# A two-layer hybrid trunk on one core: another order of the seven products, a longer estimate for accumulating loads, six output tiles by token halves, and an interleaved MLP norm

## The chip, the core and the metric

The kernel runs on one core of a Trainium2 chip. Its time is the device time of one execution in microseconds (us). Before the change, three runs took 2100.82 to 2105.32 us, median 2102.74 us.

## What is computed

The reference is one inference step of a two-layer trunk with 128 context tokens and 512 latent tokens, 640 in all, of width 1024. The part that matters here is the end of a layer: the output projection with its gated residual, the second RMSNorm with a modulation, and a squared-ReLU MLP of width 4096.

```python
def _block(x, cond, lp, lam, lam_scale, ctx):
    mod = (jax.nn.silu(cond) @ lp["w_ada"] + lp["b_ada"])[:, None, :]
    sh1, sc1, g1, sh2, sc2, g2 = jnp.split(mod, N_MOD, axis=-1)
    h = _rms_norm(x, lp["norm1_g"]) * (1 + sc1) + sh1
    m, new_kv = _mixer(h, lp, lam, lam_scale, ctx)
    x = x + g1 * m
    h = _rms_norm(x, lp["norm2_g"]) * (1 + sc2) + sh2
    f = jnp.square(jax.nn.relu(h @ lp["w_mlp1"])) @ lp["w_mlp2"]
    return x + g2 * f, new_kv
```

`_mixer` (four token mixers and their gated merge) ends in `merged @ lp["w_out"]`, and its work is not touched. Context and latent tokens have different conditioning vectors, so the modulation differs between tokens 0 to 127 and the rest.

## The kernel before

**Layout and arithmetic.** Activations are feature-major: 128 features in the partitions, 640 tokens along the free dimension, cut into two token halves of 320 (`HALVES`). Each fp32 operand is held as a rounded high part and a low part, and each product of two operands is three matmuls: high by high, low weight by high, high weight by low (`mm3`). So each weight tile of 128x1024 needs a cast on ScalarE (`whi`) and a subtraction on VectorE (`wlo`) before use, and each activation likewise (`hh` and `hl`, `p5h` and `p5l`, and so on).

**Stream of weights (`Stream`, `W`).** Weights are added in the order of use. Row 0 goes through four slots of high and low parts (`NSLOT`), row 1 through two half slots, row 2 has a buffer of its own, given with `own` (line 279). The raw data come through a ring of four raw slots; a slot is reloaded when its weights were split. `load` (240) issues a plain load on SyncE's queue and, for `more`, an accumulating load on GpSimd's queue that adds a second block of weights to the first.

**Seven products.** Three of four MLP-1 and MLP-2 steps per layer (`q` 0 to 2), and the fourth MLP-1 step, are 2x2 block products done with seven multiplications instead of eight (`square_chunks`, 540, and `block`, 2027). A product has four output tiles of 320 tokens, 48 matmuls. p1, p6, p7 and p4 add up in PSUM banks 0 to 3; p2, p5 and p3 in banks 4 to 7. p2 starts the second group, p5 starts it anew, and p3 adds to it. After each product `results` (2049) reads a group: p1, p5 and p6 are copied by ScalarE (`ev`), p2, p3 and p7 are added to such a copy by VectorE (`fq`, or `ev` in MLP-2 and the last MLP-1), p4 is read directly. The order is `ORDER` (538): p1, p2, p5, p6, p3, p7, p4. The weights of p5, p6 and p3 are sums that follow from each other: they stay in two buffers (`chain`), and each is made from the one before by one accumulating load, which is issued when the earlier one was split. p7's weights come through the raw ring, a plain load and an accumulating one.

The operands are made by `sums` (1917) from four quarters of the input, in the order p5, p6, p3, p7, p4, each waiting for units in `room` (1897). In MLP-1 the operands are used for all four `q`; those of p7 and p4 are spilled to DRAM (`put_away`, 1952) and reloaded on SyncE's queue for `q` 1 to 3 (`load_again`, 1956), called by `before` (2223) at the start of p6 (for p7) and of p3 (for p4).

**Order of work.** The order of instructions on each engine is fixed at build time by a planner that runs along with the code. `Clocks.put` (95) keeps an estimated time for each engine and buffer. A DMA is estimated by

```python
            end = max(self.t[eng], start + 1100.0) + cost(n)
        ...
        seen = end + (900.0 if eng == "dma" else self.LAG)
```

with a cost of bytes / 360 in ns. `pump` (329) puts the next weight cast in ScalarE's queue when its source is estimated to be there, and the subtraction in VectorE's. Generators in eight `lanes` hold the other work; `tick` (614), called after every two contraction steps of matmuls, steps those that are due, lower lanes first. Engines run their queues in order. `until` forces pending work when TensorE's next product has no operand.

**Units.** SBUF buffers are 30 units of 128x1280 words (`NUNIT`); a unit asked for when none is free forces pending work.

**End of a layer's first half.** The output projection has eight output tiles. `units_of` (1862) does tiles 0 to 3, each with both token halves; `tail` (828) does tiles 4 to 7 for the first half and then for the second. After each tile `x_update` adds it to the residual on VectorE and `sq_add` adds its square, ScalarE then VectorE. After each half `tail` starts `mlp_norm(part)` (1969), the first in lane 2, the second in lane 3: sums over features by TensorE (`ones`), a reciprocal square root on VectorE, a broadcast by TensorE (`ident`), a copy to `rb`, then for each of eight feature tiles a multiply on VectorE (`ht`, split at token 128 in the first half) and an activation with the shift as bias on ScalarE (`hq`); in the first half, after each pair, a cast `hh` and a subtraction `hl`, which are the operands of p1 and p2. The sums for p5 need the second half.

The trace puts every operation on one line (131), that of the wrapper, so groups are told apart by tile names.

## Time and profile before

| | |
|---|---|
| three runs | 2100.82, 2102.74, 2105.32 us |
| profiled execution | 2096.17 us |
| its span, first to last instruction | 2094.4 us |
| mean granted TensorE clock | 0.988 |
| busy: PE, DVE, ACT, POOL | 2017.3, 1325.9, 1002.9, 212.7 us |
| output projection and MLP of layer 0 | about 552 to 1030 us of the span |
| the same of layer 1 | about 1577 to 2094 us |
| HBM read | 277.92 MB |

PE is TensorE's matmuls, PEld its weight loads, DVE VectorE, ACT ScalarE, POOL GpSimd, SPq SyncE's queue. In a table of stretches each engine has its busy time and, in brackets, its number of instructions; PEclk is the granted clock. A row of waits has the total, the number of waits and the longest. A timeline row has start, duration, the instruction, and in square brackets the idle time before it and what ended it. A row of a group has the busy time, the mean ns of one, and the idle time before.

### The profile page before, as it was taken

Reading aid. Unit: us, or ns where it says so; the run is one execution under the profiler, and the core shown is the slowest. Engines: PE = TensorE matmul, PEld = TensorE weight load, DVE = VectorE, ACT = ScalarE, POOL = GpSimd, SP = SyncE. Lnnn points to the kernel's source line nnn. Section 1 sums busy time; section 2 is a strip of 40 time slices with the busy share of each in tenths; the row PEclk is TensorE's granted clock in tenths of the full one; section 3 lists DMA queues with packets and bytes.
Section 4 is the critical chain, followed back from the end, with each engine's and each line's share of the span. In section 5 each row is a group of like instructions: output and inputs, shape, how many; then the busy total and the mean of one; then the engine's idle time right before and its main releaser. Section 6 shows DMA issues by size and latency. Waiting matters only on the chain.

```text
span 2094.4 us, 35175 instructions
## 1 busy us (share of the span) xinstructions
PE 2017.3 (96%) x14404; PEld 1951.1 (93%) x14404; DVE 1325.9 (63%) x2400; ACT 1002.9 (48%) x1743; POOL 212.7 (10%) x245
## 2 busy tenths in 40 slices
PE   8999999999998999999999999999999899999998
PEld 7999999997998999998899999999889799999998
DVE  6766577863457858575467657687534676666654
ACT  4455454532236565746244544444222564646462
POOL 0000000002001122122100000000110111212100
PEclk9999999999999999999999999999999899999999
DMA  9421112347436989999331202124572488888841
GB/s 301 138 67 49 50 56 74 114 161 263 125 81 141 205 208 191 212 207 276 119 99 40 80 31 76 51 78 132 193 246 81 92 195 194 194 194 194 201 106 51
DMA packets 249762, 291.48 MB, mean 139 GB/s; under 512 B 11632, under 2 KB 214480, under 8 KB 249600
## 3 DMA queue, kind: packets, MB, share of 16 engines
q1 hardware_dynamic: 175952, 178.88, 26.6%
q0 software_dynamic: 73504, 110.29, 25.5%
q8 instruction: 113, 1.85, 0.3%
q14 instruction: 49, 0.40, 0.1%
q10 hardware_dynamic: 144, 0.07, 0.0%
HBM read 277.92 MB, written 11.27 MB: 138 GB/s over the span
## 4 chain that ended last, share of the span: by engine, by line
PE 67%; DMA 15%; DVE 8%; ACT 5%; issue 4%; POOL 1%; SPq 0%; ACTq 0%; DVEq 0%; POOLq 0%
PE psum L131 67%; DMA chain<-in_w_mlp_dram 10%; DMA raw<-in_w_mlp_dram 4%; DVE wlo L131 3%; ACT whi L131 2%; POOL raw L131 1%; DVE ev L131 1%; DVE xT L131 1%; DVE p4l L131 1%; DMA ada<-in_w_ada_dram 0%; DVE fq L131 0%; ACT ev L131 0%; DVE ht L131 0%; DMA p4s<-h_spill 0%; DVE small L131 0%
## 5 line engine op out<-in xcount | busy, mean ns | idle before, releaser
L131 DVE TENSOR_TENSOR wlo<-raw,whi 128x1024 fp32r<-128x1024 f32 (+1 forms) x274 | 315.9, 1159 | 113.7 <-ACT whi L131 110.5
L131 ACT CAST whi<-raw 128x1024 fp32r<-128x1024 f32 (+1 forms) x274 | 270.8, 997 | 118.4 <-PE psum L131 65.5
L131 PE MATMUL psum<-hhi,whi 128*128 128x320 f32 x1024 | 325.9, 318 | 0.0
L131 PE MATMUL psum<-hlo,whi 128*128 128x320 f32 x1024 | 316.5, 309 | 0.0
L131 PE MATMUL psum<-hhi,wlo 128*128 128x320 f32 x1024 | 316.3, 309 | 0.0
L131 PEld LDWEIGHTS psum<-hhi,whi 128*128 128x128 f32 x1024 | 192.5, 188 | 21.8 <-issue 19.3
L131 PE MATMUL psum<-whi,hhi 128*128 128x256 f32 x640 | 188.0, 294 | 6.3 <-DVE UV L131 4.5
L131 PEld LDWEIGHTS psum<-hhi,wlo 128*128 128x128 f32 x1024 | 192.7, 188 | 0.0
L131 PEld LDWEIGHTS psum<-hlo,whi 128*128 128x128 f32 x1024 | 192.3, 188 | 0.0
L131 DVE TENSOR_TENSOR wlo<-chain,whi 128x1024 fp32r<-128x1024 f32 x84 | 102.6, 1223 | 130.0 <-ACT whi L131 127.8
L131 PE MATMUL psum<-whi,hlo 128*128 128x256 f32 x640 | 181.5, 284 | 2.0 <-DVE hlo L131 1.8
L131 PE MATMUL psum<-wlo,hhi 128*128 128x256 f32 x640 | 180.9, 283 | 0.8 <-DVE wlo L131 0.8
L131 ACT CAST whi<-chain 128x1024 fp32r<-128x1024 f32 x84 | 88.0, 1048 | 146.0 <-DMA chain<-in_w_mlp_dram 144.9
L131 POOL DMA_DIRECT2D chain<-in_w_mlp_dram x84 | 107.9, 1285 | 400.3 <-DMA chain<-in_w_mlp_dram 230.9
L131 PEld LDWEIGHTS psum<-whi,hhi 128*128 128x128 f32 x640 | 122.0, 191 | 9.8 <-DVE UV L131 5.3
L131 PEld LDWEIGHTS psum<-whi,hlo 128*128 128x128 f32 x640 | 122.3, 191 | 3.9 <-DVE hlo L131 3.2
L131 PEld LDWEIGHTS psum<-wlo,hhi 128*128 128x128 f32 x640 | 122.1, 191 | 1.0 <-DVE wlo L131 1.0
L131 ACT ACTIVATE gt<-psum 128x320 f32<-128x320 f32 x128 | 56.1, 438 | 139.1 <-PE psum L131 139.1
L131 DVE TENSOR_REDUCE small<-psum 128x1 f32<-128x640 f32 (+1 forms) x108 | 82.2, 775 | 40.8 <-PE psum L131 38.4
L131 DVE SCALAR_TENSOR_TENSOR gt<-gt,psum 128x320 f32<-128x320 f32 x96 | 46.6, 486 | 91.9 <-PE psum L131 91.7
L131 ACT ACTIVATE sq<-xT 128x320 f32<-128x320 f32 (+2 forms) x64 | 30.1, 471 | 152.3 <-DVE xT L131 152.2
L131 PE MATMUL psum<-hl,whi 128*128 128x320 f32 x256 | 84.0, 328 | 8.2 <-DVE hl L131 8.2
(366 smaller groups left out, 5627.0 us busy)
## 6 DMA issues: line engine op xcount, KB each, us to landing
chain<-in_w_mlp_dram POOLq DMA_DIRECT2D x84, 512.0 KB, 7.1
raw<-in_w_mlp_dram SPq DMA_DIRECT2D x41, 1024.0 KB, 6.8
ada<-in_w_ada_dram POOLq DMA_DIRECT2D x80, 512.0 KB, 5.5
raw<-in_w_gate_dram SPq DMA_DIRECT2D x24, 1024.0 KB, 5.2
raw<-in_w_mlp_dram SPq DMA_DIRECT2D x46, 512.0 KB, 5.6
chain<-in_w_mlp_dram SPq DMA_DIRECT2D x28, 512.0 KB, 3.6
raw<-in_w_mlp_dram POOLq DMA_DIRECT2D x28, 512.0 KB, 7.3
raw<-in_w_in_dram SPq DMA_DIRECT2D x24, 512.0 KB, 4.8
```

Source lines behind the costliest of these rows:

```text
L131: ins = f(*args, **kw)
```

## The change

Four edits. (1) `ORDER` becomes p1, p2, p5, p6, p7, p3, p4, and the reloads of spilled operands are called at the start of p5 (for p7) and of p7 (for p4). (2) `put` adds 3500 ns to the estimated time at which an accumulating load is seen. (3) `units_of` does output tiles 0 and 1 alone, and `tail` does tiles 2 to 7, all six for the first token half and then for the second, in PSUM banks 0 to 5; the weights of tiles 2 and 3 are split into buffers of their own (`wown`, four units, row 2). (4) `mlp_norm` becomes two generators: `mlp_rstd` (lane 1) up to `rb`, and `mlp_h` (lanes 2 and 5), which multiplies two feature tiles by `rb` in one VectorE instruction, gives the scale to ScalarE's activation, and writes out the order of the steps by hand; `ht` has two more units.

```diff
-    def put(self, eng, ins, cost, reads, writes):
+    def put(self, eng, ins, cost, reads, writes, late=0.0):
...
-        seen = end + (900.0 if eng == "dma" else self.LAG)
+        seen = end + (900.0 + late if eng == "dma" else self.LAG)
...
+                            3500.0 if kw.get("accum_op") else 0.0)
...
         if s.half == 2:
+            if isinstance(s.own, tuple):
+                return s.own + (0, 0, n)
...
-    ORDER = ("p1", "p2", "p5", "p6", "p3", "p7", "p4")
+    ORDER = ("p1", "p2", "p5", "p6", "p7", "p3", "p4")
...
-            fm_chunk([("out", l, m), ("out", l, m + 1)], w_out[l], 0, m * 128)
+            fm_chunk([("out", l, m), ("out", l, m + 1)], w_out[l], 0, m * 128, half=2 if m == 2 else 0)
...
-        ss = [W.get(tag + (m,)) for m in range(4, 8)]
+        m0 = 4 if parts is PARTS else 2
+        ss = {}
...
-            for m in range(4, 8):
-                o = bank(((0, 1, 2, 3), (4, 5, 0, 1) if parts is PARTS else (4, 5, 4, 5))[part][m - 4], c1 - c0)
+            for m in range(m0, 8):
+                if m not in ss:
+                    ss[m] = W.get(tag + (m,))
+                o = bank(((0, 1, 2, 3), (4, 5, 0, 1))[part][m - 4] if m0 == 4 else m - 2, c1 - c0)
...
-        ht = kbufs("ht", n=2)
+        ht = kbufs("ht", n=4)
...
+        wown = [tuple(Buf(A, 1024, name="wown", r=True) for _ in range(2)) for _ in range(2)]
...
-        units_of(("out", l), range(4), mh, ml, ev_res(g1, True))
+        units_of(("out", l), range(2), mh, ml, ev_res(g1, True))
...
+        def mlp_h(part):
+            while part not in normed:
+                yield when(lambda: 0.0 if part in normed else NEVER)
+            r, hs = rb.f[:, part:part + 1].broadcast_to([128, 2, HN]), hs_of(part)
...
+                tt(t, two(xT[k].buf.flat_f)[:, :, hs], r, ALU.mult)
...
+                        afn(H.f[:, 2 * j + e, a:b], t[:, e, a:b], AF.Identity, scale=mulA[1].f[:, k + e, cnd:cnd + 1], bias=mods[l].f[:, 24 + k + e, cnd:cnd + 1])
...
+            for f, n in ((scaled, 0), (scaled, 1), (moved, 0), (moved, 1), (lower, 0), (scaled, 2), (moved, 2), (lower, 1), (scaled, 3), (moved, 3), (lower, 2), (lower, 3)):
+                yield from f(n)
...
+        def mlp_norm(part):
+            spawn(1, mlp_rstd(part))
+            spawn(3 * part + 2, mlp_h(part))
...
-                ahead = {"p6": "p7", "p3": "p4"}.get(P)
+                ahead = {"p5": "p7", "p7": "p4"}.get(P)
```

In the diff, `scaled` is the multiply (`ht`), `moved` the activations and, in the first half, the cast `hh`, and `lower` the subtraction `hl`.

## The prediction

> **What bounds the kernel now.** I read the page's first part, then the table of stretches, then the waits of single engines, then the timelines around the longest waits.

> ```profile
> PE 2017.3 (96%) x14404; PEld 1951.1 (93%) x14404; DVE 1325.9 (63%) x2400; ACT 1002.9 (48%) x1743; POOL 212.7 (10%) x245
> ```

> TensorE is busy 96% of the span, so a change that removes no matmul can win only what TensorE loses by idling or by a lower clock. The next table cuts out the first four products of each MLP (one row for each layer), then the rest of its seven-product blocks.

> ```profile
> core 0: us, PE busy (x) PEld busy (x) DVE busy (x) ACT busy (x) POOL busy (x), PEclk, DMA share, GB/s
> 610.90:661.50 50.60, 39.91 (x215) 37.44 (x213) 34.94 (x63) 30.01 (x50) 7.66 (x6) 0.80 0.55 105
> 1636.30:1687.50 51.20, 40.62 (x214) 38.02 (x213) 34.95 (x63) 30.04 (x50) 9.90 (x8) 0.77 0.58 112
> 661.50:986.60 325.10, 317.94 (x2162) 316.77 (x2161) 229.75 (x290) 192.75 (x245) 67.31 (x60) 1.00 0.92 214
> 1687.50:2023.00 335.50, 322.17 (x2162) 317.03 (x2161) 229.33 (x290) 191.51 (x246) 59.44 (x47) 1.00 0.84 188
> ```

> The last two rows hold 45 products of 48 matmuls each. The weight loads of the third row, 316.77 us, are the undisturbed work: 7.04 us a product, 3.52 us for half an output tile (24 matmuls). So the body loses 325.1 - 316.8 = 8.3 us in layer 0 and 335.5 - 316.8 = 18.7 us in layer 1.

> The first four products ought to take 4 x 7.04 = 28.2 us. Between them lie two small groups of the norm, which the timeline has once each while the clock was full (the first and third row here):

> ```profile
> 597.26 0.74 PE L131 MATMUL psum<-ones,sq 128*64 128x1 f32 x10
> 604.77 0.42 ACT L131 COPY rb<-psum 128x320 f32<-128x320 f32 x1 [1.08 <-PE psum L131]
> 603.40 1.33 PE L131 MATMUL psum<-ident,small 64*128 64x64 f32 x10
> 612.75 0.74 PE L131 MATMUL psum<-ones,sq 128*64 128x1 f32 x10 [1.67 <-DVE sq L131]
> 633.69 0.82 DVE L131 TENSOR_TENSOR hl<-hq,hh 128x640 fp32r<-128x640 f32 x1
> 650.79 1.04 ACT L131 CAST whi<-chain 128x1024 fp32r<-128x1024 f32 x1 [1.58 <-DMA chain<-in_w_mlp_dram]
> ```

> That makes 30.2 us of work in stretches of 50.6 and 51.2 us: 20.4 and 21.0 us lost. In all 20.4 + 21.0 + 8.3 + 18.7 = 68.4 us are within the change's reach. Who is waited for in the start of layer 0:

> ```profile
> PE psum L131 <- DVE hl L131: 4.1, 2, 3.6
> PE psum L131 <- ACT p6h L131: 2.7, 1, 2.7
> PE psum L131 <- ACT hh L131: 2.1, 2, 1.3
> PE psum L131 <- DVE sq L131: 1.7, 1, 1.7
> ```

> These are 10.6 us; the other half is clock (granted 0.80 over 50.6 us costs 10.1 us). hh and hl are the first token half's normalised input, sq its sum of squares; the last hl comes at 634.51, 30 us after rb; the norm of the second half ran in between. In the bodies, layer 0 (two rows), then layer 1:

> ```profile
> PE psum L131 <- DVE fq L131: 3.8, 2, 3.4
> PE psum L131 <- DVE ev L131: 3.4, 3, 2.2
> ```
> ```profile
> PE psum L131 <- DVE ev L131: 6.1, 6, 1.7
> PE psum L131 <- DVE wlo L131: 4.6, 6, 0.8
> ```

> Two engines queue behind accumulating loads. ScalarE's own waits in the two bodies, layer 0 and then layer 1:

> ```profile
> ACT whi L131 <- DMA chain<-in_w_mlp_dram: 57.6, 21, 7.3
> ```
> ```profile
> ACT whi L131 <- DMA chain<-in_w_mlp_dram: 72.3, 24, 7.9
> ```

> One such wait close up, ScalarE and then VectorE:

> ```profile
> 748.72 1.05 ACT L131 CAST whi<-chain 128x1024 fp32r<-128x1024 f32 x1 [7.34 <-DMA chain<-in_w_mlp_dram]
> ```
> ```profile
> 743.26 0.82 DVE L131 TENSOR_TENSOR fq<-ev,psum 128x640 f32<-128x640 f32 x1 [0.62 <-PE psum L131]
> 749.80 1.22 DVE L131 TENSOR_TENSOR wlo<-chain,whi 128x1024 fp32r<-128x1024 f32 x1 [5.72 <-ACT whi L131]
> 752.71 0.81 DVE L131 TENSOR_TENSOR fq<-ev,psum 128x640 f32<-128x640 f32 x1
> ```

> The cast of p6's weights stood 7.34 us in ScalarE's queue for a DMA, VectorE's subtraction of the same weights behind it, and behind that the addition fq that reads p2's banks; p5 writes those banks, and TensorE waited 3.4 us.

> **Longer estimate.** The planner lets a 512 KB load be seen 1100 + 1456 + 900 = 3456 ns after its start. The DMA view says what accumulating ones take:

> ```profile
> chain<-in_w_mlp_dram POOLq DMA_DIRECT2D x84, 512.0 KB, 7.1
> p4s<-h_spill SPq DMA_DIRECT2D x6, 640.0 KB, 9.4
> ```

> With 3500 ns more it is 6.96 us against 7.1, so the cast is put in ScalarE's queue near the landing, behind the relu and squares that now wait for it. The p5 waits (fq 3.8 and 2.2 of ev in layer 0) should go. Nothing is added to any queue.

> [...]

> **Order.** p7 adds into p6's banks, p4 into p7's. With p3 between p7 and p4, VectorE's read of p7 (ev) has 7.04 us more: the ev waits before p4 (1.2 us of layer 0, 6.1 of layer 1) go. p3's weights, the last link of three accumulating loads, are needed 7.04 us later: most of wlo's 4.6 us goes. p7's weights are a ring load independent of that chain. Their GpSimd loads keep their place, ahead of p6's in POOL's queue. New constraints: p7 directly behind p6 needs ScalarE's copy of p6 within 3.52 us, which hides as long as no cast waits ahead of it; and p7's operand is needed 7.04 us earlier. Where it stood in the six MLP-2 blocks, as stretches from p6's last matmul to p7l's first half (first, last and sum of six):

> ```profile
> 710.80:715.30 4.50, 0.00 (x0) 0.00 (x0) 0.78 (x2) 1.00 0.47 129
> 1944.40:1950.60 6.20, 0.00 (x0) 0.00 (x0) 0.82 (x2) 1.00 0.55 158
> sum 24.60, PE 0.00 PEld 0.00 DVE 4.87; mean PE 0.00 PEld 0.00 DVE 0.81
> ```

> Left where it is, p7's operand would cost 24.6 us. But ScalarE and VectorE make it behind the same blocked casts (57.6 + 72.3 us over 14 blocks, 9.3 us a block against 4.1 us of lateness). Bounds 0 and 24.6; I take 4, near the lower end, since the release exceeds the lateness. The reload of p7's spilled operand moves one product earlier in SP's queue, ahead of the next chain's first loads; p4's goes behind the first of them, lands 9.4 us after issue, and may cost a microsecond or two in layer 1.

> Body: layer 0 keeps about 2 of 8.3 (the sum of unlisted small waits), gain 6.3. Layer 1 keeps about 8 of 18.7 (p6's weights still land late, p4's reload), gain 10.7. Less 4 for p7: 13.0 net, bounds 0 (p7 at 17) and 24 (of 27.0 lost).

> **Six tiles by halves.** The same matmuls and updates run in another order: six half tiles instead of four stand between the end of the first half and the first product, 21.1 us instead of 14.1 of cover. The casts for two of the tiles go into four extra units; their price is that of any cast, 1.04 us, at the same place.

> **Interleaved norm.** Prices, VectorE and then ScalarE:

> ```profile
> L131 DVE SCALAR_TENSOR_TENSOR ht<-xT,mulA,rb 128x320 f32<-128x320 f32 x8 | 4.1, 548 | 2.5 <-ACT hq L131 1.7 <-ACT rb L131 0.9
> L131 DVE SCALAR_TENSOR_TENSOR ht<-xT,mulA,rb 128x192 f32<-128x192 f32 x8 | 3.3, 410 | 0.0
> L131 DVE TENSOR_TENSOR hl<-hq,hh 128x640 fp32r<-128x640 f32 x4 | 3.3, 816 | 0.0
> L131 DVE SCALAR_TENSOR_TENSOR ht<-xT,mulA,rb 128x128 f32<-128x128 f32 x8 | 2.8, 352 | 1.0 <-ACT rb L131 1.0
> ```
> ```profile
> L131 ACT ACTIVATE hq<-ht,mods 128x320 f32<-128x320 f32 x8 | 4.2, 559 | 1.5 <-DVE ht L131 1.5
> L131 ACT ACTIVATE hq<-ht,mods 128x192 f32<-128x192 f32 x8 | 3.6, 445 | 0.0
> L131 ACT CAST hh<-hq 128x640 fp32r<-128x640 f32 x4 | 2.9, 725 | 0.1
> L131 ACT ACTIVATE hq<-ht,mods 128x128 f32<-128x128 f32 x8 | 3.2, 399 | 1.9 <-DVE ht L131 1.9
> L131 ACT ACTIVATE sq<-xT 128x320 f32<-128x320 f32 x4 | 1.9, 470 | 7.0 <-DVE xT L131 7.0
> ```

> VectorE's 24 multiplies (4.1 + 3.3 + 2.8 = 10.2 us) become eight of 128x640, 8 x 0.82 = 6.6 us by the nearest row: 3.6 less a layer. ScalarE's 24 activations take a scale operand more; the rows 559 against 470 ns (one operand more) bound that at 0 to 89 ns each, 2.1 us a layer; I take 0, since a constant scale was applied before too.

> From the first half's sums (597.26) to rb's end (605.19) takes 7.9 us. ScalarE then has 3.6 + 3.2 + 2.9 = 9.7 us for the first half and, beside it, squares and weight casts. In 21.1 + 2 us of cover that nearly fits: p1's operands are ready when the tail ends, p2's about then. hl's 4.1, hh's 2.1 and most of sq's 1.7 us go. p6h's 2.7 us go with the estimate: at 650.79 its cast stood behind a waiting chain cast.

> What is late next is VectorE. It worked 34.94 us in this stretch. Of the first half's 6.1 + 3.3 = 9.4 us I put 7 (estimate) ahead of the stretch, the second half saves 1.1, and p7's operand, now fifth, adds four of 0.82: 34.9 - 7.0 - 1.1 + 3.3 = 30.1 us, as long as TensorE's own 30.2. At the 69% that VectorE reached there the stretch would take 43.6 us, at 95% it would take 31.7. I take 37, the middle: dependences p5, p6, p3, p7 are serial, but TensorE stands less. Gain 13.6 and 14.2, together 27.8 (bounds 14.6 and 38.4).

> The 6.8 us that 37 leaves over 30.2 hold some 2 us of slow clock. The trace grants 0.80 where the longest wait was 3.6 us, 1.00 in the body with one of 3.4. [...]

> **Sum.** 13.0 + 27.8 = 40.8 us. The profiled execution took 2096.17 us, 6.57 less than the median 2102.74 of the runs shown; from it, 2055.4. From the median: 2102.74 - 40.8 = 2061.9, so 2062.

> **Rivals.**
> - All hidden: both upper bounds, 38.4 + 24 = 62.4 us, 2040. For it: VectorE idles 29% of the bodies. Against: the serial sums.
> - VectorE binds the start: the stretch stays at 43.6 us, gain 14.6 + 13 = 27.6, 2075. For it: 30.1 us of work in 30.2.
> - The change doesn't do what it says: free slots, and not the estimate, place the casts. Then layer 0's 6.0 us at p5 and p7's remaining 20.6 stay: 2062 + 26.6 = 2089. Against: p6's slot was free long before 748.72, since the cast already stood waiting.
> - The estimate is too long: casts stand 3.5 us late in layer 1's seven blocks, where the weights are waited for: at most 24.5 us, 2086. [...]
> - Slower: p7 waits for its operand in all six MLP-2 blocks, 24.6 us as traced, and the slow clock doubles it as at the start (10.1 us for 10.6 of waits): 48. Gains of 14.6 at the start and 17 in the bodies leave 2102.74 + 48 - 31.6 = 2119. It decides from a mean wait of 2.7 us a block (31.6 / 1.95 / 6). For it: p7 is now directly behind p6; against: granted clock 1.00 in every body.

> **Chances.** Forecast (2050 to 2071) 0.50; all hidden 0.19; VectorE binds 0.12; no new order of casts 0.06; estimate too long 0.02; slower 0.08; gains and p7's wait cancelling 0.03. A measurement tells about 0.2%, 4 us, from no change: faster 0.89, same 0.03, slower 0.08. The range takes in the forecast, most of all hidden, VectorE's case and half of the next: 2040 to 2086.

> **What would show it.** Right: PEclk near 1.00 in the first four products, which take about 37 us with p7 instead of p3 after them; no PE wait for hl or hh; ScalarE's chain waits well under half of 57.6 and 72.3; no PE wait for ev ahead of p4. Wrong: PE waits for p7h or p7l over 2 us a block; chain waits as long as before; a start stretch over 44 us; waits in the out projection, which has none to spare.

## The result, and the profile after

The changed kernel takes **2069.41 us** (median of 4 runs, 2068.32 to 2073.53) against 2104.03 us for the kernel before on the same chip (4 runs, 2100.82 to 2108.20). The ratio is 0.9838, 95% interval 0.9815 to 0.9861: 34.6 us or 1.6% faster, against 40.8 us (2062) predicted. The profiled execution of the changed kernel ran 2070.21 us with a span of 2068.4 us; that of the kernel before had a span of 2094.4 us. Between the two spans lie only 26.0 us, because the profiled execution of before was 7.9 us below its median and that of after 0.8 us above. What follows accounts for the 26.0 us; the other 8.6 us lie between executions and have no place in the two traces.

The first line of the page, as before, now reads:

```profile
PE 2009.4 (97%) x14404; PEld 1949.1 (94%) x14404; DVE 1322.5 (64%) x2370; ACT 1009.0 (49%) x1741; POOL 212.9 (10%) x245
```

VectorE issues 30 instructions fewer: sixteen large multiplies stand in place of 48 small ones, and two copies (brD) went from ScalarE to it. The table of stretches answers to the one in the prediction: first the four products at the start of each MLP, then the bodies, then the two stretches between the body of layer 0 and the out projection of layer 1.

```profile
core 0: us, PE busy (x) PEld busy (x) DVE busy (x) ACT busy (x) POOL busy (x), PEclk, DMA share, GB/s
612.10:648.60 36.50, 32.69 (x215) 31.64 (x214) 30.16 (x48) 28.09 (x42) 6.41 (x5) 0.95 0.76 142
1634.70:1672.70 38.00, 34.20 (x215) 33.09 (x214) 30.22 (x48) 28.07 (x42) 7.74 (x6) 0.91 0.77 156
648.60:969.70 321.10, 318.71 (x2161) 318.18 (x2160) 227.71 (x286) 187.89 (x238) 68.04 (x60) 0.99 0.91 210
1672.70:1996.60 323.90, 320.47 (x2161) 319.68 (x2160) 231.39 (x291) 194.98 (x246) 61.78 (x48) 0.99 0.87 200
969.70:1049.70 80.00, 70.61 (x462) 60.87 (x461) 36.50 (x81) 26.78 (x46) 10.85 (x20) 0.96 0.50 167
1049.70:1576.10 526.40, 515.96 (x3822) 495.99 (x3821) 326.49 (x673) 227.43 (x485) 24.54 (x47) 1.00 0.30 99
```

The last two of these stretches were, in the kernel before:

```profile
986.60:1056.80 70.20, 67.24 (x461) 58.82 (x460) 33.38 (x78) 22.80 (x40) 10.32 (x19) 1.00 0.46 151
1056.80:1577.70 520.90, 513.94 (x3824) 494.38 (x3823) 323.54 (x670) 227.10 (x486) 26.94 (x48) 1.00 0.31 100
```

Read the two tables side by side. The start stretches fell from 50.6 and 51.2 to 36.5 and 38.0 us (-14.1 and -13.2), the bodies from 325.1 and 335.5 to 321.1 and 323.9 (-4.0 and -11.6). But two stretches that the change doesn't touch grew: layer 0's last MLP-2 and the tail behind it from 70.2 to 80.0 us, at a clock of 0.96 instead of 1.00, and the attention of layer 1 from 520.9 to 526.4 us. They give back 15.3 us. The part ahead of layer 0's out projection took 1.2 us more (552.2 and 553.4), the end of the kernel 0.4 more; the out projections (58.7 and 58.6) stayed. The sum is -14.1 - 13.2 - 4.0 - 11.6 + 15.3 + 1.6 = -26.0.

TensorE's waits in the start of layer 0, in the view of waits (the fifth product is included):

```profile
PE psum L131 <- DVE small L131: 2.1, 1, 2.1
PE psum L131 <- DVE p7l L131: 1.8, 1, 1.8
PE psum L131 <- DVE p5l L131: 1.7, 2, 1.4
```

hl, hh, sq and p6h, 10.6 us together before, are gone; what is left is VectorE, in the rstd's chain of small operations (small) and in the operands p5l and p7l. ScalarE's waits for accumulating loads, in the body of layer 0 and in that of layer 1:

```profile
ACT whi L131 <- DMA chain<-in_w_mlp_dram: 23.3, 12, 4.3
```
```profile
ACT whi L131 <- DMA chain<-in_w_mlp_dram: 20.8, 11, 5.7
```

They were 57.6 and 72.3 us. So far the steps came as forecast. The rest of the document is about three things that they don't explain: what each part did alone, and the two stretches that grew.

### The profile page after: what moved, and what is told of

Read it like the earlier page. It is cut to its first block, busy times and chain, and to the rows that moved or that the text cites. A ratio compares the mean times of both kernels' runs of the same rounds, so it can differ in the third digit from the quotient of the medians.

```text
span 2068.4 us, 35108 instructions
## 1 busy us (share of the span) xinstructions
PE 2009.4 (97%) x14404; PEld 1949.1 (94%) x14404; DVE 1322.5 (64%) x2370; ACT 1009.0 (49%) x1741; POOL 212.9 (10%) x245
## 3 DMA queue, kind: packets, MB, share of 16 engines
q1 hardware_dynamic: 175952, 178.88, 26.6%
## 4 chain that ended last, share of the span: by engine, by line
PE 90%; DVE 3%; DMA 2%; ACT 2%; SPq 2%; issue 1%; DVEq 0%; ACTq 0%
PE psum L131 90%; SPq L131 2%; DMA raw<-in_w_mlp_dram 1%; DMA p4s<-h_spill 1%; DMA raw<-in_w_gate_dram 1%; DVE wlo L131 1%; ACT whi L131 0%; DVE small L131 0%; DMA ada<-in_w_ada_dram 0%; DVE UV L131 0%; ACT UV L131 0%; DVE hq L131 0%; ACT L131 0%; DVE p5l L131 0%; DVE ht L131 0%
## 5 line engine op out<-in xcount | busy, mean ns | idle before, releaser
L131 DVE TENSOR_TENSOR wlo<-raw,whi 128x1024 fp32r<-128x1024 f32 (+1 forms) x270 | 311.7, 1158 | 131.3 <-ACT whi L131 129.6
L131 ACT CAST whi<-raw 128x1024 fp32r<-128x1024 f32 (+1 forms) x270 | 268.1, 995 | 153.2 <-PE psum L131 97.7
L131 PE MATMUL psum<-hhi,whi 128*128 128x320 f32 x1024 | 326.5, 319 | 0.1
L131 PE MATMUL psum<-hlo,whi 128*128 128x320 f32 x1024 | 317.0, 310 | 0.0
L131 PE MATMUL psum<-hhi,wlo 128*128 128x320 f32 x1024 | 316.8, 309 | 0.0
L131 PEld LDWEIGHTS psum<-hhi,whi 128*128 128x128 f32 x1024 | 193.0, 189 | 24.5 <-issue 21.8
L131 PE MATMUL psum<-whi,hhi 128*128 128x256 f32 x640 | 188.1, 294 | 6.3 <-DVE UV L131 4.5
L131 PEld LDWEIGHTS psum<-hhi,wlo 128*128 128x128 f32 x1024 | 193.3, 189 | 0.0
L131 PEld LDWEIGHTS psum<-hlo,whi 128*128 128x128 f32 x1024 | 192.8, 188 | 0.0
L131 PE MATMUL psum<-whi,hlo 128*128 128x256 f32 x640 | 181.6, 284 | 2.3 <-DVE hlo L131 2.0
L131 PE MATMUL psum<-wlo,hhi 128*128 128x256 f32 x640 | 180.8, 283 | 0.8 <-DVE wlo L131 0.8
L131 POOL DMA_DIRECT2D chain<-in_w_mlp_dram x84 | 108.0, 1290 | 435.0 <-DMA chain<-in_w_mlp_dram 225.9
L131 DVE TENSOR_TENSOR wlo<-chain,whi 128x1024 fp32r<-128x1024 f32 x84 | 102.2, 1223 | 73.8 <-ACT whi L131 73.3
L131 PEld LDWEIGHTS psum<-whi,hhi 128*128 128x128 f32 x640 | 122.0, 191 | 9.8 <-DVE UV L131 5.3
L131 ACT ACTIVATE gt<-psum 128x320 f32<-128x320 f32 x128 | 56.1, 438 | 151.7 <-PE psum L131 148.7
L131 PEld LDWEIGHTS psum<-whi,hlo 128*128 128x128 f32 x640 | 122.3, 191 | 4.6 <-DVE hlo L131 4.0
L131 PEld LDWEIGHTS psum<-wlo,hhi 128*128 128x128 f32 x640 | 122.1, 191 | 1.0 <-DVE wlo L131 1.0
L131 ACT CAST whi<-chain 128x1024 fp32r<-128x1024 f32 x84 | 87.7, 1049 | 44.1 <-DMA chain<-in_w_mlp_dram 44.1
L131 DVE TENSOR_REDUCE small<-psum 128x1 f32<-128x640 f32 (+1 forms) x108 | 82.4, 775 | 38.2 <-PE psum L131 36.4
L131 DVE SCALAR_TENSOR_TENSOR gt<-gt,psum 128x320 f32<-128x320 f32 x96 | 46.7, 486 | 88.5 <-PE psum L131 87.7
L131 ACT ACTIVATE sq<-xT 128x320 f32<-128x320 f32 (+2 forms) x64 | 30.0, 471 | 142.4 <-DVE xT L131 142.3
L131 ACT COPY ev<-psum 128x640 f32<-128x640 f32 x84 | 58.1, 692 | 70.9 <-PE psum L131 67.1
## 6 DMA issues: line engine op xcount, KB each, us to landing
chain<-in_w_mlp_dram POOLq DMA_DIRECT2D x84, 512.0 KB, 7.2
ada<-in_w_ada_dram POOLq DMA_DIRECT2D x80, 512.0 KB, 6.1
raw<-in_w_mlp_dram SPq DMA_DIRECT2D x46, 512.0 KB, 5.8
chain<-in_w_mlp_dram SPq DMA_DIRECT2D x28, 512.0 KB, 4.3
raw<-in_w_mlp_dram POOLq DMA_DIRECT2D x28, 512.0 KB, 7.6
raw<-in_w_in_dram SPq DMA_DIRECT2D x24, 512.0 KB, 4.6
```

The source lines that it names most:

```text
L131: ins = f(*args, **kw)
```

## Experiments

All of them are compared with the kernel before on the same chip. In the table the stages run from the first matmul of one to the first of the next, by the traces: out projection and start together (from the first out-projection matmul to the fifth product), the body (from the fifth product to the last MLP-2 part), what lies behind it in layer 0 (to the first attention matmul of layer 1), and layer 1's attention. Each row of stages is one profiled execution, and the executions of one kernel lie up to 14 us apart (order alone, 12 runs), so a microsecond or two in a stage is not read as an effect.

| kernel | ratio to before (95%) | out + start, layer 0 / 1 | body 0 / 1 | behind body 0 | attention 1 |
|---|---|---|---|---|---|
| before | 1 | 109.3 / 109.8 | 325.1 / 335.5 | 70.2 | 520.9 |
| order alone | 0.9970 (0.9958 to 0.9983) | 109.7 / 108.4 | 334.5 / 327.8 | 71.1 | 520.9 |
| estimate alone | 1.0088 (1.0070 to 1.0106) | 104.7 / 104.8 | 347.1 / 353.0 | 68.2 | 520.8 |
| order and estimate | 0.9897 (0.9880 to 0.9914) | 107.9 / 107.8 | 318.5 / 321.7 | 80.3 | 520.8 |
| six tiles and norm | 0.9912 (0.9894 to 0.9930) | 97.8 / 96.3 | 327.1 / 337.0 | 70.0 | 526.0 |
| after, with the old norm | 0.9896 (0.9882 to 0.9909) | 102.2 / 103.0 | 324.1 / 320.7 | 80.0 | 526.0 |
| after, with four tiles | 0.9880 (0.9864 to 0.9896) | 103.0 / 102.9 | 320.4 / 322.2 | 79.8 | 520.9 |
| after | 0.9838 (0.9815 to 0.9861) | 95.1 / 96.5 | 321.3 / 324.1 | 79.9 | 526.4 |

### The parts: order, estimate, start

The first kernel is the one before with the new order alone:

```
-    ORDER = ("p1", "p2", "p5", "p6", "p3", "p7", "p4")
+    ORDER = ("p1", "p2", "p5", "p6", "p7", "p3", "p4")
...
-                ahead = {"p6": "p7", "p3": "p4"}.get(P)
+                ahead = {"p5": "p7", "p7": "p4"}.get(P)
```

> The kernel before with the new order of the products (and of the reloads that go with it) alone. Theory (the prediction's: the estimate makes the new order pay): casts still stand in ScalarE's queue ahead of their DMAs (chain waits near 57.6 and 72.3 us), so p7, now directly behind p6, waits for its operand in most of the six MLP-2 blocks, 4.1 us a block in the mean, 24.6 us in all; against it stand the ev waits (7.3 us) and wlo (4.6 us) that go: 2104 + 24.6 - 12 = 2117 or, with some clock lost, up to 2125. Rival 1 (the order does the work in the bodies, the estimate adds little): both bodies shrink by 12 to 15 us as in the changed kernel, 2090. For the loss after layer 0's MLP (969.8 to 994.5 us in the changed kernel, about 10 us): if the reload of p4 at its new place is the cause, it is here too; if the shift of the schedule by the new start is the cause, it isn't.

Measured: 2095.98 us, 0.3% faster. Neither side is right as a whole. TensorE's waits for p7's operand, in the body of layer 1:

```profile
PE psum L131 <- DVE p7l L131: 4.8, 5, 1.4
PE psum L131 <- ACT ev L131: 1.9, 3, 0.8
PE psum L131 <- ACT p7h L131: 1.4, 1, 1.4
```

With 1.4 and 0.4 us in layer 0 that is 8.0 us over both layers, a third of the 24.6 us that the prediction took from where the casts stood before: when the product moves, the planner places its operand's casts anew. Layer 0 lost at p5 instead (fq, 6.2 us). ScalarE still waited 36.0 and 27.1 us for the chain, but that is 21.6 and 45.2 us less than before, by the order alone.

The second has the estimate alone:

```
-        seen = end + (900.0 if eng == "dma" else self.LAG)
+        seen = end + (900.0 + late if eng == "dma" else self.LAG)
...
+                            3500.0 if kw.get("accum_op") else 0.0)
```

> The kernel before with the longer estimate alone. Theory (prediction): ScalarE's chain waits fall well under half of 57.6 and 72.3 us, the p5 waits of layer 0 (6.0 us) and p6h's 2.7 in the start go, layer 1's body keeps its ev and wlo waits in part: 8 to 14 us faster, 2090 to 2096. Rival 1 (the order does the work): within 3 us of the kernel before, 2101 to 2107. Rival 2 (the estimate is too long): casts late where the weights are the last to come, up to 24 us slower, 2128. The loss after layer 0's MLP isn't here if the reload of p4 at its new place causes it, and is here if the estimate (casts and subtractions put later, raw loads issued later) causes it.

Measured: 2121.4 us, 0.9% **slower**; the theory falls. ScalarE's waits for the chain did fall, to 13.1 us in layer 0, but both bodies grew, to 347.1 and 353.0 us. TensorE's waits in layer 0's body, with the old order, name another pair:

```profile
PE psum L131 <- ACT whi L131: 8.5, 5, 1.7
PE psum L131 <- DVE wlo L131: 7.1, 10, 1.3
```

One of these waits close up, ScalarE first and then TensorE (start, duration, instruction, and in brackets how long the engine stood and for whom):

```profile
705.39 0.69 ACT L131 COPY ev<-psum 128x640 f32<-128x640 f32 x1
708.91 0.69 ACT L131 COPY ev<-psum 128x640 f32<-128x640 f32 x1 [2.83 <-PE psum L131]
709.50 1.05 ACT L131 CAST whi<-chain 128x1024 fp32r<-128x1024 f32 x1
```
```profile
708.56 0.31 PE L131 MATMUL psum<-p6l,whi 128*128 128x320 f32 x1
710.60 0.41 PE L131 MATMUL psum<-p3h,whi 128*128 128x320 f32 x1 [1.73 <-ACT whi L131]
711.86 0.53 PE L131 MATMUL psum<-p3h,wlo 128*128 128x320 f32 x1 [0.85 <-DVE wlo L131]
```

The cast at 709.50 is that of p3's weights, the last of the three accumulating links. Its row has no wait for a DMA: its data had landed. With the longer estimate the planner puts it behind the copy of p6's sums (708.91), and that copy waits for p6's last matmul. In the old order p3 follows p6 at once, so TensorE stands from the end of p6 until the cast and the subtraction are through, in ten of the fourteen blocks, and its matmuls run slowly for some microseconds after (0.53 instead of 0.31 us). So the cast that stood waiting in ScalarE's queue before was in the way of others, but it was also the one that was needed first. In the new order p7, whose weights are plain ring loads, stands between p6 and p3, and the same late cast is in time.

The third kernel joins the two edits, and nothing else is changed:

```
+                            3500.0 if kw.get("accum_op") else 0.0)
...
+    ORDER = ("p1", "p2", "p5", "p6", "p7", "p3", "p4")
...
+                ahead = {"p5": "p7", "p7": "p4"}.get(P)
```

> Order and estimate together, the start as before (four tiles by halves, the norm as before). Theory (prediction): the two together gain the 13.0 us of the bodies that the prediction gave them (0 to 24): 2091; the two start stretches stay at 50 to 51 us less p6h's 2.7. Rival (the parts are not separate: the body's gain came from the better start, which brings the waiting casts and the spilled operands forward): less than 5 us gained. If the loss after layer 0's MLP comes from order or estimate, it stands here too and the sum is 2098 to 2104.

Measured: 2079.81 us. The bodies gain 6.6 and 13.8 us, 20.4 together instead of 13.0, where order alone had cost 1.7 net and the estimate alone 39.5. The two are no separate terms: each needs the other. In the table the loss behind layer 0's body (80.3 us) comes with the pair as well, and with neither part alone.

The fourth is the changed kernel with the old order and the old estimate, so six tiles and the interleaved norm alone:

```
-                            3500.0 if kw.get("accum_op") else 0.0)
+                            0.0 if kw.get("accum_op") else 0.0)
...
-    ORDER = ("p1", "p2", "p5", "p6", "p7", "p3", "p4")
+    ORDER = ("p1", "p2", "p5", "p6", "p3", "p7", "p4")
...
-                ahead = {"p5": "p7", "p7": "p4"}.get(P)
+                ahead = {"p6": "p7", "p3": "p4"}.get(P)
```

> Six tiles by halves and the interleaved norm, with the old order and the old estimate. Theory (prediction): the two start stretches (four products p1, p2, p5, p6) gain 27.8 us less what the estimate gave to p6h (2.7) and with p3 for p7 as the fifth product: 2104 - 25 = 2079; bodies as before (325 and 335 us). Rival (the parts are not separate: without the estimate, ScalarE's blocked casts stand inside the start, whose norm then comes late): the start stretches stay over 43 us, 2090 or more. The loss after layer 0's MLP: here if the shift of the schedule is its cause, not here if order or estimate is.

Measured: 2083.42 us. Out projection and start gain 11.5 and 13.5 us, 25.0 in all, as expected, and the bodies stay near those of before (+2.0, +1.5). Stage by stage the parts nearly add, with the pair of order and estimate as one of them: out projection and start gain 25.0 and 3.4 us alone and 27.5 in the changed kernel, the bodies -3.5 and 20.4 alone and 15.2 there, by the table. By the medians they gain 19.4 and 23.1 us alone and 34.6 together; no run shows where the 7.9 us between go. The attention of layer 1 is 5.1 us longer: that loss belongs to the start's edits.

Two more split the start. The first leaves the six tiles and has the function mlp_norm of before, spawned as before:

```
-        tail(("out", l), g1, mh, ml, mlp_norm, HALVES)
+        tail(("out", l), g1, mh, ml, lambda part: spawn(2 + part, mlp_norm(part)), HALVES)
```

> The changed kernel with the MLP norm of before (one token half after the other, each tile multiplied, activated, cast and subtracted in turn; 24 multiplies instead of 8) behind the six-tile tail. Theory (prediction: the cover of 7 us more does most for the first half's operands, the interleaving and 3.6 us less of VectorE work do the rest): the start stretches, 36.4 and 37.9 us with both edits and 46.7 with neither, come out at 40 to 43 us, so 2076 to 2082. Rival 1 (cover is all): 37 to 38 us, 2070. Rival 2 (the order of the norm is all: hl comes last because the second half's work stands ahead of it): 45 to 47 us, 2086.

The second has the new norm behind the old four-tile tail, without the wown buffers:

```
-        m0 = 4 if parts is PARTS else 2
+        m0 = 4
...
-        units_of(("out", l), range(2), mh, ml, ev_res(g1, True))
+        units_of(("out", l), range(4), mh, ml, ev_res(g1, True))
```

> The changed kernel with the four-tile tail of before and the interleaved norm: 14.1 us of cover in place of 21.1. Out projection and start together took 109.3 and 109.8 us before, 107.9 and 107.8 with order and estimate only, 102.2 and 103.0 with six tiles and the old norm, 95.1 and 96.5 in the changed kernel. Theory (the two edits add: six tiles 5 to 6 us, the norm 7 us a layer): 100.5 to 102 us in each layer, so the kernel 10 to 12 us slower than the changed one, 2080, less what the attention stretch of layer 1 gives back (5 us, if the six tiles' units and not the norm shifted its schedule). Rival (they only work together, since with 14 us of cover the first operands come late whatever the order): 105 us or more, 2085 to 2090.

Measured: 2080.93 and 2076.84 us. With order and estimate in all of them, out projection and start take 107.9 and 107.8 us with neither edit, 102.2 and 103.0 with six tiles, 103.0 and 102.9 with the norm, 95.1 and 96.5 with both. Alone they bring 5.7 and 4.8 (tiles) or 4.9 and 4.9 us (norm), together 12.8 and 11.3: they add, with about 2 us more. The expectations were a little too good: 100.5 to 102 for the norm alone, and a start of 40 to 43 us for the tiles alone, where it took 43.5 and 44.4. No run takes the norm's edit apart, its eight multiplies from its order of steps. The attention of layer 1 is 526.0 us with six tiles and 520.9 with four: its loss comes with the tiles, not with the norm.

### The loss behind layer 0's body

ScalarE's longest wait of this place, then its queue, then GpSimd's waits, in the changed kernel:

```profile
ACT p4h L131 <- DMA p4s<-h_spill: 9.6, 1, 9.6
```
```profile
948.55 1.05 ACT L131 CAST whi<-chain 128x1024 fp32r<-128x1024 f32 x1
959.17 1.36 ACT L131 CAST p4h<-p4s 128x640 fp32r<-128x640 f32 x2 [9.57 <-DMA p4s<-h_spill]
960.43 1.04 ACT L131 CAST whi<-raw 128x1024 fp32r<-128x1024 f32 x1
...
966.84 1.03 ACT L131 CAST whi<-raw 128x1024 fp32r<-128x1024 f32 x1
```
```profile
POOL ada L131 <- ACT ev L131: 14.9, 1, 14.9
```

p4's spilled operand lands 13.7 us after its issue (945.43 on SP). Its cast was put into ScalarE's queue 9.6 us too early and holds everything behind it: the raw casts, after which the next raw loads start, and the activations on whose buffers the modulation loads of layer 1 (ada, 512 KB each) wait on GpSimd. Then nine of them start within 8 us:

```profile
964.01 3.13 POOL L131 DMA_DIRECT2D ada<-in_w_ada_dram  x6 [14.89 <-ACT ev L131]
970.42 1.57 POOL L131 DMA_DIRECT2D ada<-in_w_ada_dram  x3 [3.29 <-DVE ev L131]
```

The next raw load, a pair of tiles of the last MLP-2 part (1024 KB), is issued among them, at 966.10. ScalarE then stands for it until 981.29 (the row is shown below), 15.2 us after the issue, and TensorE, which entered that part at 969.8, stands behind ScalarE's operand fhi:

```profile
983.02 0.63 PE L131 MATMUL psum<-fhi,whi 128*128 128x320 f32 x1 [4.57 <-ACT fhi L131]
```

Two causes are possible, the blocked cast or the competing loads, and four kernels ask which. One has a longer estimate for the reloads:

```
-    3500.0 if kw.get("accum_op") else 0.0)
+    3500.0 if kw.get("accum_op") else 6000.0 if getattr(kw.get("out"), "name", "")[:3] in ("p7s", "p4s") else 0.0)
```

> The changed kernel with one edit: the planner's estimate for the reloads of the two spilled operands (640 KB on SP's queue) is 6000 ns longer (9.8 us from start instead of 3.8; 9.4 measured in the kernel before, 13.7 for the one in question). ScalarE's casts p4h and p7h are put later in its queue, the transfers keep their order. The loss in question: layer 0's last MLP-2 and the tail behind it took 79.9 us in the changed kernel against 70.2 before, 80.3 with order and estimate, 71.1 and 68.2 with one of them alone. Theory (a cast of p4's spilled operand that is put into ScalarE's queue 9.6 us before its data land holds back the casts of raw weights, so the next raw loads start late and TensorE waits): p4h's wait falls from 9.6 to about 4 us, the stretch falls to 70 to 75 us, the kernel 5 to 10 us faster than the changed one, 2060 to 2065. Rival (twelve loads of layer 1's modulation on GpSimd's queue compete with the raw loads there): the stretch stays at 79 to 80 us, the time within 3 us of 2069. Second rival: p4's operand, now cast late, is waited for in the other blocks: up to 2 us in each of six, 2069 to 2081.

One has p4's reload a product earlier:

```
-                ahead = {"p5": "p7", "p7": "p4"}.get(P)
+                ahead = {"p5": "p7", "p6": "p4"}.get(P)
```

> The changed kernel with p4's reload issued one product earlier (at p6 instead of p7). Same loss, other way to take the cause away: the data land before the cast is put into the queue. Theory (blocked cast): p4h's wait goes, the stretch of 79.9 us falls to about 70 us, 2059 to 2064. Rival (competing loads): stays at 79 to 80 us. Against it in any case: the reload now stands ahead of p5's and p6's successors in the queues and shares the DMA engines with them, which can cost a few us in the bodies (321.3 and 324.1 us).

One leaves out twelve of the modulation loads, and its products use the first two loads' data in their place:

```
+        if (l, s) == (1, 0) and k < 6:
+            ada_in[l, s, k + 2] = ada_in[l, s, k]
...
-            if i + 2 < len(steps):
+            if i + 2 < len(steps) and (l, s) != (1, 0):
```

> The changed kernel without 12 of the 16 loads (512 KB each) of the first third of layer 1's modulation weights: its products use the first two loads' data eight times over, which leaves out that part of the computation. The matmuls stay. Theory (blocked cast): p4h's wait stays at 9 to 10 us, and the stretch after layer 0's seven-product blocks stays within 3 us of 79.9 us. Rival (competing loads): the raw loads land as early as before and the stretch falls to 70 us. If both have a share, it lies between.

And one joins the first two:

> The changed kernel with both edits of the reloads: p4's reload one product earlier (at p6) and the planner's estimate for both reloads 6000 ns longer. With the estimate alone the stretch after layer 0's seven-product blocks fell from 79.9 to 68.3 us, but p4's operand came 3.1 us late in two blocks (body of layer 0 321.3 -> 331.7); with the earlier reload alone p4's cast stood in ScalarE's queue ahead of the copy of p6's sums and TensorE waited at p7 (4.0, 2.0 and 7.1 us; body 338.0). Theory (one cause in all three: a cast that stands in ScalarE's queue for a reload that hasn't landed, or one that is put there too late for its product): with 7 us more lead and an estimate near the landing both waits go: body of layer 0 at 319 to 323 us, the stretch at 68 to 71 us, the kernel 8 to 12 us under the changed one, 2057 to 2062. Rival (the earlier reload itself costs: it shares the DMA engines with the chain's loads and delays p6's or p3's weights): body of layer 0 at 328 us or more, 2066 to 2072.

| kernel | time, ratio (95%) | body 0 / 1 | behind body 0 | attention 1 |
|---|---|---|---|---|
| reload's estimate | 2066.58, 0.9825 (0.9811 to 0.9839) | 331.7 / 324.1 | 68.3 | 526.8 |
| reload earlier | 2071.03, 0.9848 (0.9825 to 0.9870) | 338.0 / 322.1 | 68.2 | 524.4 |
| no modulation loads | 2055.52, 0.9773 (0.9757 to 0.9790) | 321.4 / 324.1 | 68.7 | 525.0 |
| both edits of the reload | **2057.98, 0.9792 (0.9777 to 0.9806)** | 319.0 / 324.5 | 70.7 | 526.3 |

Without the loads the wait for p4's data was nearly as long, and the loss was gone all the same (here the wait, then the stretch):

```profile
ACT p4h L131 <- DMA p4s<-h_spill: 7.3, 1, 7.3
```
```profile
970.10:1038.90 68.80, 66.15 (x462) 59.45 (x461) 35.02 (x79) 25.51 (x44) 3.80 (x7) 1.00 0.38 125
```

So a cast blocked for 7.3 us costs TensorE nothing without the loads; the expectation that it would is wrong. But with all the loads and the cast blocked for 3.3 us (reload's estimate) or 2.8 (both edits) the loss is gone too. With the reload earlier the cast stood even 10.5 us, but it was through 21 us before TensorE entered the part, and the loss was gone as well. How that fits shows in ScalarE's cast of that 1024 KB pair, in the changed kernel, without the modulation loads, and with both edits of the reload. In all three ScalarE waits for the data, so the start of the cast is their landing:

```profile
981.29 1.04 ACT L131 CAST whi<-raw 128x1024 fp32r<-128x1024 f32 x1 [7.53 <-DMA raw<-in_w_mlp_dram]
```
```profile
974.69 1.05 ACT L131 CAST whi<-raw 128x1024 fp32r<-128x1024 f32 x1 [1.94 <-DMA raw<-in_w_mlp_dram]
```
```profile
969.05 1.05 ACT L131 CAST whi<-raw 128x1024 fp32r<-128x1024 f32 x1 [3.44 <-DMA raw<-in_w_mlp_dram]
```

The pair's load was issued at 966.10, 965.10 and 957.88: 3.7, 5.0 and 7.8 us before TensorE entered the part (969.8, 970.1, 965.7). It took 15.2, 9.6 and 11.2 us, so it landed 11.5, 4.6 and 3.4 us into the part. Unblocking the cast issues the load 4.1 us earlier and shortens it by 4.0; taking the competing loads away shortens it by 5.6. Either is enough, since TensorE has other tiles for the first microseconds. All fourteen traces agree: in the four with the loss (the changed kernel, order and estimate, old norm, four tiles) the pair was issued 3.7 us before the part and landed 11.4 to 12.0 us into it; in the ten others it was issued 5.0 to 13.4 us before and landed at most 4.6 us into it. That the blocked cast also bunches the loads is read from GpSimd's waits for them (14.9 us for ScalarE in the changed kernel; with both edits none for ScalarE and 7.7 us at most); no run took that link apart by itself.

Each half of the repair alone made a new wait, in layer 0's body; only that of the first half had been foreseen, as its second rival. With the estimate alone, p4's cast came too late for its product; with the earlier reload alone, p4's cast was put in ahead of the copy of p6's sums, and TensorE waited for that copy at p7. The two waits, in this order:

```profile
PE psum L131 <- ACT p4h L131: 6.1, 2, 3.1
```
```profile
PE psum L131 <- ACT ev L131: 13.1, 3, 7.1
```

Alone, neither half is distinguishable from the changed kernel. With both edits neither wait occurs. That kernel is faster than both given ones: 2057.98 us, its interval clear of the changed kernel's.

### The attention of layer 1

In the attention of layer 1 the changed kernel has one wait that the kernel before has not. VectorE's part in the changed kernel, with TensorE's transposes behind it:

```profile
1475.90 0.17 DVE L131 TENSOR_TENSOR ctxR<-ctxR 128x10 f32<-128x10 f32 x1
1477.01 0.49 DVE L131 SCALAR_TENSOR_TENSOR gt<-gt,psum 128x320 f32<-128x320 f32 x1 [0.93 <-PE psum L131]
1477.53 0.49 DVE L131 TENSOR_TENSOR acc<-acc,gt 128x320 f32<-128x320 f32 x1
1477.94 0.16 DVE L131 TENSOR_TENSOR ctxR<-ctxR 128x10 f32<-128x10 f32 x1
1478.13 0.17 DVE L131 SCALAR_TENSOR_TENSOR ctxR<-ctxR 128x10 f32<-128x10 f32 x1
1478.34 0.82 DVE L131 TENSOR_TENSOR OC<-OC,ctxR 128x640 f32<-128x640 f32 x1
1479.19 0.82 DVE L131 TENSOR_TENSOR OC<-OC,csm 128x640 f32<-128x640 f32 x1
```
```profile
1480.08 0.81 PE L131 MATMUL psum<-ident,OC 128*128 128x128 f32 x5 [3.18 <-DVE OC L131]
```

In the kernel before the transposes found OC ready:

```profile
1480.79 0.71 PE L131 MATMUL psum<-ident,OC 128*128 128x128 f32 x5
```

A chain of small operations is cut two before its end by the read of a gate tile (gt, acc), for which VectorE waits until TensorE has made it. The transposes of the chain's result stand in TensorE's queue where the planner expected OC to be ready, 3.2 us too early. Two kernels try to move them (on top of both edits of the reload):

```
-            yield pe_at([OC.f], [PS[:, TB:TB + T]])
+            yield (lambda: max(clk.ready(OC.f), clk.free(PS[:, TB:TB + T])) + 4000.0), ()
```

> The kernel of the expectation before with one edit more: in the attention's normalisation of branch C the transposes of OC are put into TensorE's queue 4000 ns of the planner's time later. In the changed kernel they stood there 3.18 us before VectorE had OC ready (layer 1, 526.4 us for the stretch against 520.9 before; 526.0 with the start's edits alone, 520.8 and 520.9 with order and estimate). Theory (the new start shifted the planner's times so that the last two small operations of the chain fell behind a read of a gate tile which TensorE had yet to make, and the transposes were put ahead of both): that wait goes, the stretch falls by 4 to 6 us to 520 to 522, the kernel 4 to 6 us faster than the one before it. Rival (the branch's result is needed at once, so the wait moves to the cast bh or the tile after it): the stretch stays at 525 to 527, the time within 2 us.

The other has `+ 4000.0 * l`, so layer 1 alone:

> The kernel with both edits of the reloads (2058.0 us) and the later transposes in layer 1 alone. With the later transposes in both layers, layer 1's attention fell from 526.3 to 522.9 us, but the same wait of 3.17 us for OC stood in layer 0 instead, where the stretch ahead of the out projection rose from 551.6 to 558.7. Theory (whether the transposes meet an unfinished OC is a matter of how the planner's times fall against the gate tiles, pair of heads by pair of heads): left alone, layer 0 is at 551 to 553 us without a wait for OC, layer 1 at 521 to 523, the kernel 3 to 5 us faster than 2058, 2053 to 2055. Rival (the later transposes of layer 1 also shift its MLP, as the delay did elsewhere): start and body of layer 1 rise by as much as the attention gives, 2056 to 2060.

Measured: 2060.88 us (0.9801, 0.9783 to 0.9819) and 2058.34 us (0.9785, 0.9770 to 0.9800); neither is distinguishable from the 2057.98 us without it. The wait for OC goes from layer 1 in both and the attention falls to 522.9 and 523.5 us. But with the delay in both layers the same wait stood in layer 0:

```profile
PE psum L131 <- DVE OC L131: 3.2, 1, 3.2
```

and the stretch ahead of its out projection rose from 551.6 to 558.7 us. In the last kernel no OC wait is left, and its profiled execution is the shortest of all (span 2051.0), yet the median did not follow. What is shown: this wait stands in layer 1 in all seven kernels that have six tiles and unmoved transposes, and in none of the five with four tiles. What is read from the rows and not shown: that it is a matter of where the planner's times fall against the gate tiles. What is open: which of the six tiles' edits (buffers, casts, half tiles) shifts the planner's times, and a repair that holds.

## Why the prediction was right, and where its steps were not

**The size.** 2062 against 2069.4, inside the range and faster as said. Of the miss 6.2 us are gain (34.6 instead of 40.8) and 1.3 us the median of before, which came out at 2104.03 instead of 2102.74. That it is so small is partly luck. By the profiled executions the gain is 26.0 us, 14.8 short: the two losses outside the change's reach are 15.3 us, of which the prediction had none (its "microsecond or two" stood for p4's reload in layer 1), 1.6 us were lost ahead of and behind the stages and 0.5 in the starts, while the bodies gave 15.6 us instead of 13.0. The 8.6 us between the executions made up for more than half of that.

**What bounds it.** Right: the matmuls are the same 14404, the busy weight loads stayed at 1949.1 us (1951.1 before), and what was won or lost is TensorE's waits and slow clock.

**The start.** Forecast 37 us, measured 36.5 and 38.0; gain 27.8 forecast, 27.3 measured. Its reasons hold in the main: no wait for hl or hh, PEclk 0.95 and 0.91 where it said near 1.00, VectorE late next with 30.2 us of work in the stretch (30.1 forecast), no waits added in the out projection (58.7 us, as before). That 30.2 meets 30.1 is partly luck. By the durations of the instructions 5.4 us of the first half's work went ahead of the stretch and not 7, the fifth product's operand added nothing and not 3.3, since its sums had stood there already and p7l comes after the stretch, while a sum for p4 (0.8 us) and one more split of weights (1.2 us) fell into it. The wait for sq was that for the second half's squares (TensorE's matmul at 612.75; the first half's is the one at 597.26), not for the first's; it went, and 2.1 us for the second half's rstd (small) came. "VectorE binds the start" at 43.6 us did not happen with both edits; with either alone the stretch took 43.5 to 44.4 us (the table's values less 58.7 us of out projection).

**The longer estimate.** Its effect on ScalarE is as said, though not its alone (57.6 to 23.3, 72.3 to 20.8 us with both; 36.0 and 27.1 by the order, 13.1 and 5.7 by the estimate; no p5 waits in the changed kernel's bodies). The step that failed is "Nothing is added to any queue", and with it the sum of two separate terms: the cast is moved behind a copy that waits for TensorE, and only the new order gives the time for that. "The estimate is too long" got a chance of 0.02; with the old order it is what happens (+18.5 us by medians). On the transfer itself the prediction's reading stands: the accumulating loads took 7.2 us from issue to landing in the changed kernel, 7.1 before, in bodies where the DMA engines are busy 0.91 and 0.87 of the time (0.92 and 0.84 before).

**The order.** For p7's operand, needed 7.04 us earlier, the prediction said "Bounds 0 and 24.6; I take 4". It was near: in the MLP-2 blocks, for which the 4 us stood, the changed kernel has no wait for it. Outside them the fifth product of each layer waits 1.8 and 1.7 us: the function `sums` still makes the operands in the old order, so VectorE does p3l and a sum for p4 (3.1 us, from 644.32 and from 648.40 us in layer 0) ahead of p7l (649.87). No run moved them. The upper end was far off, since even without the estimate it cost 8.0 us. So the slower rival, p7 waiting 24.6 us and more, did not come about: it took the casts' old places for fixed, where the planner places them anew.

**p4's reload.** The step "lands 9.4 us after issue, and may cost a microsecond or two in layer 1" failed in size and place. It landed after 13.7 us in the block where modulation loads run beside it, and its blocked cast, together with these loads, cost 9.8 us in layer 0; in layer 1 TensorE waited 1.7 us for p4l.

**Outside the reach.** The prediction added terms only where the diff acts. This planner derives every later position from its running times, so a change of one stage re-deals the queues of all that follow; here one wait of 3.18 us, 5.5 us with the slow clock and what else moved.

**The clock.** The prediction kept some 2 us of slow clock in the start, an estimate. The traces have 0.05 of 36.5 us, which is 1.8, and 0.09 of 38.0, which is 3.4, with no wait over 2.1 us. The longest wait doesn't explain them: the prediction set 0.80 with one of 3.6 us beside 1.00 with one of 3.4, and here 0.95 and 0.91 both stand with 2.1 us. The last section has more.

## What to carry to other kernels

A planner's estimate and the order of the work are one choice: a truthful duration moves a conversion behind other work in its queue (here p3's cast, at 709.50 us behind a copy for which ScalarE had stood 2.83 us), so look at what it is now queued behind and whether the consumer has a product of slack, before counting the removed wait as gain. A spilled operand that is reloaded needed both here, lead in issue and an honest landing time; half of the repair moved the wait to a neighbour (6.1 us for p4h, 13.1 us for ev). And in a kernel whose queues come from one running plan, look for new waits in the stages behind the edit, not only in the edited one.

## What the runs showed of the hardware that was not expected

In these traces the length of a TensorE wait doesn't tell what clock it costs. Here are one product of the kernel before with a wait of 3.41 us in it, the product behind a wait of 1.76 us in the changed kernel, and one behind waits of 1.73 and 0.85 us with the estimate alone (PEclk is the third number from the end):

```profile
746.50:757.20 10.70, 7.29 (x50) 7.06 (x49) 4.74 (x5) 6.95 (x10) 2.56 (x2) 1.00 0.76 117
```
```profile
648.50:659.10 10.60, 8.84 (x50) 8.58 (x49) 7.67 (x9) 5.43 (x7) 1.30 (x2) 0.84 1.00 296
```
```profile
708.60:720.30 11.70, 9.12 (x50) 8.64 (x50) 7.69 (x8) 5.63 (x6) 2.57 (x2) 0.85 0.64 173
```

The longest of the three cost no clock; the others cost 0.16 of 10.6 us (1.7) and 0.15 of 11.7 us (1.8) on top of themselves. What differs between these waits is their place. From 560 us on, the traces of the kernel before and of the changed one hold two granted clocks, 1.00 and 0.50, and in each the slow stretches begin on one grid of 3.41 us: those of the changed kernel between 600 and 1000 us at 623.92, 651.22 and 982.32 us, which are 8 and 97 steps of 3.41 us apart. Here are the stretch of this grid that holds the 1.76 us wait and the one after it, then the two that hold the wait of 3.41 us:

```profile
647.81:651.22 3.41, 1.65 (x12) 1.39 (x11) 3.41 (x5) 1.57 (x3) 0.00 (x0) 1.00 1.11 290
651.22:654.64 3.42, 3.42 (x15) 3.42 (x14) 2.90 (x4) 1.72 (x3) 1.07 (x1) 0.50 0.94 288
```
```profile
748.38:751.80 3.42, 1.88 (x13) 1.62 (x12) 1.22 (x1) 3.02 (x4) 0.48 (x1) 1.00 0.62 98
751.80:755.21 3.41, 1.54 (x11) 1.57 (x12) 2.69 (x3) 2.66 (x5) 1.05 (x2) 1.00 0.60 84
```
